# The down projection of a gated MLP written as seven products of halves (Strassen) in place of one direct product

## The chip, the cores and the metric

One core of one Trainium2 chip. The metric is the device time of one execution in microseconds (us). The engines are named as in the profile: PE is the matrix engine (PEld its weight loads), DVE the vector engine, ACT the scalar engine, POOL the GpSimd engine, SP the engine that issues nearly all transfers.

## The reference

One layer of a hybrid token mixer followed by a gated MLP with a depthwise convolution, for 512 tokens of 1024 channels, in fp32. The part that matters here is the second half:

```python
def conv_ffn(h, p):
    u, g = jnp.split(h @ p['ffn_w_up'], 2, axis=-1)
    g = depthwise_conv(g, p['ffn_conv_w'], p['ffn_conv_b'])
    return (jax.nn.silu(g) * u) @ p['ffn_w_down']
...
x = x + gate2 * conv_ffn(ada_norm(x, norm2_g, shift2, scale2), p)
out = rmsnorm(x, final_norm_g)
```

(the last two lines are shortened.) `ffn_w_up` is 1024 x 5632, `ffn_w_down` is 2816 x 1024. So the down projection is a product of 512 x 2816 activations with 2816 x 1024 weights.

## The kernel before, in words

All fp32 products are made of three matmuls of a rounded type: each operand x is split into a high part (a cast on ACT) and a low part (x minus the high part, on DVE), and high-high, high-low and low-high are added in PSUM (`mm3`, L99; `split`, L95). A weight tile is loaded by SP into one of 2 raw buffers and split into one of 3 buffers for each part (`load_split`, L84), so the split of a tile waits until PE has read the tile three places ahead of it.

The MLP starts at L996. The normalised input is kept channel by channel as `hxh` and `hxl` (L179), 8 tiles of 128 channels x 512 tokens each, and the residual stream as 8 tiles `xt` in the same layout. The **up projection** makes 44 tiles of 128 hidden channels (22 of `g`, 22 of `u`), each of 8 x 3 matmuls of 512 columns (`up`, L1015). The first three tiles (L1023) are done by token halves, since the second half of the input is ready later. For each of the 22 hidden tiles (loop at L1032), the convolution reads the `g` tile (one ACT and two DVE instructions), SiLU follows on ACT, the `u` tile is multiplied in on DVE, and the result is split into `act`. Accumulators are in PSUM: 4 banks for large products (tag `big`: `pup`, `pdn` and others) and 4 for all others (tag `ps`) (L74).

The **down projection** (loop at L1045) goes over 8 tiles of 128 output channels. Weights are the stationary operand, the 512 tokens of `act` stream past:

```python
1045        for mt in range(KT):
...
1050            for hs in ((full,) if mt < KT - 1 else halves):
1051                p = ps("pdn")[:, hs]
1052                for k in range(NF):
1053                    wh, wl = ws[k // KT]
1054                    w = slice((k % KT) * P, (k % KT + 1) * P)
1055                    mm3(p, wh[:, w], wl[:, w], act[k][:, 0, hs], act[k][:, 1, hs], k == 0, k == NF - 1)
```

That is 7 tiles of 22 x 3 matmuls of 512 columns and one, the last, of 2 x 22 x 3 of 256 columns. After each tile the residual is added, its squares are summed over the tiles (`ssq`), the final norm's gain is multiplied in (`xg`), and PE transposes the tile to token rows (`pxt`, 4 transposes), which ACT copies into `xo` (4 tiles of 128 tokens x 1024 channels). At the end each token half has its sum of squares formed by PE (`pst`), a chain of small instructions gives the reciprocal root, and the rows are scaled and stored (4 transfers of 512 KB, L1081).

The order of the instructions on each engine is set by a planner when the kernel is built: the program text gives priorities, and an instruction may move ahead of earlier ones that are not ready by the planner's own costs. Stretches marked `pinned` keep the order of the text. Transfers issued by one engine go out in that engine's order, and one that waits holds up those behind it.

Of the kernel before, what the change touches and what calls it, by code (L numbers as in the profile page):

```python
# [14 lines left out]
P = 128  # L15
# [6 lines left out]
EPS = 1e-6  # L22
FH = 2816
NF = FH // P
GW = 64
RW = 63

# [12 lines left out]
INV2PI = 1.0 / (2 * math.pi)  # L40
MAGIC = 1.5 * 2.0 ** 23
PI_LO = 3.1415925
CUT = 576


@with_exitstack
def block_kernel(ctx: ExitStack, tc: tile.TileContext, A):
# [47 lines left out]
    def split(hi, lo, src):  # L95
        S.copy(hi, src)
        V.tensor_sub(lo, src, hi.bitcast(F32))
# [18 lines left out]
    def col(name, i=0, n=1):  # L116
        o = COLS[name][0] + i
        return cols[:, o:o + n]
# [877 lines left out]
    with ExitStack() as ff:  # L996
        fp = ff.enter_context(tc.tile_pool(name="ffn", bufs=1))
        h2h, h2l = hxh, hxl

        def tmp(n):  # L1000
            return yslot("hm", dt=F32)[:, 0, :n]

        for h, hs in enumerate(halves):
            if h:
                norm2_cols(h)
                norm2_rows(h)
            for k in range(KT):
                modulate(tmp, h2h[:, k, hs], h2l[:, k, hs], xt[k][:, hs], rb2[h], a2col[:, k:k + 1], modc[:, 8 + k:9 + k])
        act = []
# [12 lines left out]

        first = {}  # L1023
        for m in (NF, 0, NF + 1):
            first[m] = (load_split(A["wup"][m], name="wup"), ps("pup"))
        for hs in halves:
            for ms in ((NF, 0), (NF + 1,)):
# [4 lines left out]
        for f in range(NF):  # L1032
            pg = first[NF + f][1] if NF + f in first else up(NF + f)
            gt = fp.tile([P, T], F32, name="gt", tag="gt", bufs=2)
# [8 lines left out]
        xo = fp.tile([P, 4, D], F32, name="xo")  # L1043
        tmp = temp(fp)
        for mt in range(KT):  # L1045
            ws = []
            for c in range(0, NF, KT):
                n = min(KT, NF - c)
                ws.append(load_split(A["wdn"][mt, :, c * P:(c + n) * P], n * P, name="wdn"))
            for hs in ((full,) if mt < KT - 1 else halves):  # L1050
                p = ps("pdn")[:, hs]
                for k in range(NF):
                    wh, wl = ws[k // KT]
                    w = slice((k % KT) * P, (k % KT + 1) * P)
                    mm3(p, wh[:, w], wl[:, w], act[k][:, 0, hs], act[k][:, 1, hs], k == 0, k == NF - 1)
                V.scalar_tensor_tensor(xt[mt][:, hs], p, modc[:, 24 + mt:25 + mt], xt[mt][:, hs], ALU.mult, ALU.add)
                n = hs.stop - hs.start
                if mt < KT - 1:
                    sumsq(tmp, ssq[:, hs], xt[mt][:, hs], mt == 0)
                else:  # L1060
                    sq = tmp(n)
                    S.activation(sq, xt[mt][:, hs], AF.Square)
                xg = fp.tile([P, T], F32, name="xg", tag="gt", bufs=2)[:, hs]
                V.tensor_scalar(xg, xt[mt][:, hs], col("final", mt), None, ALU.mult)
                tt = range(4)[hs.start // P:hs.stop // P]
                if mt == KT - 1:
                    r = rms_cols(sum_cols(ssq[:, hs], sq))
                pt = ps("pxt")[:, hs]
                for i in range(len(tt)):
                    PE.transpose(pt[:, i * P:(i + 1) * P], xg[:, i * P:(i + 1) * P], ident)  # L1070
                if mt == 4:
                    preload_sqrt(ssq[:, 0:1])
                if mt < KT - 1:
                    S.copy(xo[:, tt.start:tt.stop, mt * P:(mt + 1) * P], pt.rearrange("p (t c) -> p t c", c=P))
                    continue
                for i, t in enumerate(tt):
                    rt = r[:, i:i + 1]
                    V.tensor_scalar(xo[:, t, :CUT], xo[:, t, :CUT], rt, None, ALU.mult)
                    S.mul(xo[:, t, CUT:mt * P], xo[:, t, CUT:mt * P], rt)
                    V.tensor_scalar(xo[:, t, mt * P:], pt[:, i * P:(i + 1) * P], rt, None, ALU.mult)  # L1080
                    nc.sync.dma_start(A["out"][t * P:(t + 1) * P], xo[:, t])  # L1081

# [52 lines left out]
def _arrays(x, c, ctx, c_ctx, w_mod, b_mod, norm1_g, norm2_g, w_in, pool_w, pool_scale,  # L1135
            hyena_conv_w, hyena_conv_b, hyena_filt_w1, hyena_filt_b1, hyena_filt_w2,
            hyena_filt_b2, hyena_filt_w3, hyena_filt_b3, hyena_freq, hyena_skip, na_rpb,
            w_branch, w_out, ffn_w_up, ffn_conv_w, ffn_conv_b, ffn_w_down, final_norm_g):
    import numpy as np
    a = _constants()  # L1140

    def tcol(v):
        return v.reshape(-1, P).T

    def chan(m):
        return m.T.reshape(KT, P, -1).transpose(1, 0, 2)
# [20 lines left out]
    a["wdn"] = mtiles(ffn_w_down[0])  # L1167
# [46 lines left out]
```

## Time and profile before

| | us |
|---|---|
| median of 3 runs | 855.87 (855.58 to 857.28) |
| the profiled execution | 855.23 |
| its span, first to last instruction | 853.4 |
| mixer and output projection | up to about 475 |
| MLP, up projection | about 475 to 718 |
| MLP, down projection | 718 to 843.5 |
| from there to the end | 9.9 |

PE is busy 832.1 of the 853.4 us, DVE 502.6, ACT 332.1. Matmuls are pipelined: the duration shown for one (376 ns on average) is longer than the step from one to the next, so what PE can do is read from start to start, or from a long unbroken stretch and its count. The same holds in a smaller measure for instructions of DVE.

### The profile page before, as it was taken

The page shows a single profiled execution, that of the slowest core. Times are in us where ns is not written, and L with a number is a line of the kernel's source. Part 1 is how long each engine was busy: PE and PEld are TensorE (multiplying, and loading weights), DVE is VectorE, ACT ScalarE, POOL GpSimd, SP SyncE. Part 2 cuts the span into 40 slices and gives each one's busy share as a digit, 9 for nine tenths or more (in the row PEclk, how much of TensorE's full clock was granted, in tenths as well). Part 3 has the DMA queues.
Part 4 walks back from the last instruction along what each step waited for, and adds up shares of the span by engine and source line. Part 5 has one row for each costly group of instructions (what it writes and reads, how often), then busy time and mean ns, then how long its engine had stood idle before and what let it go on. Part 6 is the DMA issues. An engine that isn't in the chain of part 4 may idle for free.

```text
span 853.4 us, 10736 instructions
## 1 busy us (share of the span) xinstructions
PE 832.1 (97%) x4192; PEld 683.8 (80%) x4192; DVE 502.6 (59%) x874; ACT 332.1 (39%) x519; POOL 5.9 (1%) x16
## 2 busy tenths in 40 slices
PE   6999999989999999999999999999999999999995
PEld 2577888868888888888889988888888888888885
DVE  4879998699797863445444964444444444232333
ACT  6634452625454332323333453333333333222321
POOL 0100000000000000000000000000000000000000
PEclk9999999999999999999999999999999999999998
DMA  8912314645656542223332233222222333332312
GB/s 315 414 60 74 99 44 140 190 144 208 210 166 220 185 158 93 93 93 130 113 122 76 74 124 99 98 97 92 91 96 95 99 99 93 87 107 84 93 57 99
DMA packets 30363, 107.31 MB, mean 126 GB/s; under 512 B 3783, under 2 KB 4935, under 8 KB 29288
## 3 DMA queue, kind: packets, MB, share of 16 engines
q1 hardware_dynamic: 30312, 106.62, 37.6%
q8 instruction: 33, 0.54, 0.3%
q14 instruction: 18, 0.15, 0.0%
HBM read 104.51 MB, written 2.10 MB: 125 GB/s over the span
## 4 chain that ended last, share of the span: by engine, by line
PE 86%; DVE 8%; ACT 2%; DMA 1%; issue 1%; SPq 0%; DVEq 0%; ACTq 0%
PE pup L60 28%; PE pin L60 25%; PE pdn L60 14%; PE pwo L60 5%; PE pbr L60 5%; PE pss L60 1%; DVE za L60 1%; PE pKe L60 1%; PE pav L60 1%; DVE winl L60 1%; DVE zb L60 1%; PE pmod L60 1%; DMA cb<-in_crow_dram 1%; DMA wm<-in_wmB_dram 1%; DVE wgl L60 1%
## 5 line engine op out<-in xcount | busy, mean ns | idle before, releaser
L60 PE MATMUL pup<-hxh,wupl 128*128 128x512 f32 (+1 forms) x376 | 140.8, 376 | 0.0
L60 PE MATMUL pup<-hxl,wuph 128*128 128x512 f32 (+1 forms) x376 | 140.6, 376 | 0.0
L60 PE MATMUL pup<-hxh,wuph 128*128 128x512 f32 (+1 forms) x376 | 139.9, 376 | 0.7 <-ACT wuph L60 0.4
L60 PE MATMUL pdn<-act,wdnh 128*128 128x512 f32 (+1 forms) x396 | 112.7, 368 | 0.0
L60 PE MATMUL pin<-hxh,wgh 128*128 128x512 f32 x256 | 101.2, 395 | 0.6 <-ACT wgh L60 0.6
L60 PE MATMUL pin<-hxh,wgl 128*128 128x512 f32 x256 | 100.3, 392 | 0.0
L60 PE MATMUL pin<-hxl,wgh 128*128 128x512 f32 x256 | 100.2, 391 | 0.0
L60 DVE TENSOR_TENSOR wupl<-wupr,wuph 128x1024 fp32r<-128x1024 f32 x44 | 53.9, 1225 | 71.7 <-ACT wuph L60 69.8
L60 ACT CAST wuph<-wupr 128x1024 fp32r<-128x1024 f32 x44 | 46.3, 1053 | 92.6 <-PE pup L60 90.2
L60 PEld LDWEIGHTS pdn<-act,wdnh 128*128 128x128 f32 x396 | 71.6, 189 | 12.0
L60 PEld LDWEIGHTS pup<-hxh,wupl 128*128 128x128 f32 x376 | 70.7, 188 | 13.1 <-DVE wupl L60 0.2
L60 PEld LDWEIGHTS pup<-hxh,wuph 128*128 128x128 f32 x376 | 70.1, 188 | 13.7 <-ACT wuph L60 0.6
L60 PEld LDWEIGHTS pup<-hxl,wuph 128*128 128x128 f32 x376 | 70.6, 188 | 12.8
L60 PE MATMUL pdn<-act,wdnl 128*128 128x512 f32 (+1 forms) x198 | 72.4, 366 | 0.0
L60 DVE TENSOR_TENSOR wdnl<-wdnr,wdnh 128x1024 fp32r<-128x1024 f32 (+1 forms) x24 | 27.2, 1134 | 63.3 <-ACT wdnh L60 63.2
L60 ACT ACTIVATE sg<-pin 128x512 f32<-128x512 f32 x32 | 19.2, 600 | 113.5 <-PE pin L60 113.4
L60 DVE SCALAR_TENSOR_TENSOR sg<-sg,pbr 128x512 f32<-128x512 f32 x24 | 16.5, 689 | 75.8 <-PE pbr L60 75.8
L60 PEld LDWEIGHTS pin<-hxh,wgh 128*128 128x128 f32 x256 | 48.1, 188 | 10.5 <-ACT wgh L60 1.0
L60 PEld LDWEIGHTS pin<-hxh,wgl 128*128 128x128 f32 x256 | 48.1, 188 | 10.3 <-issue 0.5
L60 PEld LDWEIGHTS pin<-hxl,wgh 128*128 128x128 f32 x256 | 48.1, 188 | 9.8 <-issue 0.5
L60 ACT CAST wdnh<-wdnr 128x1024 fp32r<-128x1024 f32 (+1 forms) x24 | 23.6, 983 | 72.5 <-PE pdn L60 66.7
L60 PE MATMUL pin<-hxh,winh 128*128 128x512 f32 x128 | 51.7, 404 | 0.0
(265 smaller groups left out, 1427.5 us busy)
## 6 DMA issues: line engine op xcount, KB each, us to landing
wupr<-in_wup_dram SPq DMA_DIRECT2D x44, 512.0 KB, 3.4
wgr<-in_wg_dram SPq DMA_DIRECT2D x32, 640.0 KB, 3.9
wm<-in_wmB_dram SPq DMA_DIRECT2D x32, 512.0 KB, 4.6
wm<-in_wmA_dram SPq DMA_DIRECT2D x8, 1024.0 KB, 9.9
winr<-in_win_dram SPq DMA_DIRECT2D x16, 512.0 KB, 3.5
wdnr<-in_wdn_dram SPq DMA_DIRECT2D x16, 512.0 KB, 3.5
wor<-in_wout_dram SPq DMA_DIRECT2D x8, 512.0 KB, 3.5
wdnr<-in_wdn_dram SPq DMA_DIRECT2D x8, 384.0 KB, 3.1
```

The lines of the kernel that those rows point to most:

```text
L60: ins = f(*a, **k)
```

## The change

The hidden channels are halved (11 tiles each), the tokens are halved (2 x 256) and the output channels are halved (2 x 512). Seven products of 256 x 1408 by 1408 x 512 take the place of the eight of the direct form. In each, 128 x 128 blocks of the activations are the stationary operand, and 512 columns of the weights stream past; a product fills two PSUM banks (two blocks of 128 tokens). Write A for the first hidden half and B for the second, 1 and 2 for the token halves, W11 to W22 for the quarters of the weights (hidden half, output half).

- p7: (A1 - A2) with W12 + W22. p6: (A2 - B2 - A1) with W12 + W22 + W11. p4: B2 with the sum of all four. These three run hidden tile by hidden tile beside the up projection (`part`, taken by `run_part` from a queue `todo` between the up tiles: three per pair of hidden tiles, from the second pair on). The summed weights of a hidden tile lie in one buffer (`chain`): one transfer on SP loads W12, three transfers issued by POOL each add a quarter to it in memory; two of the three are issued after the sum so far has been split.
- p1: A1 with W11. p5: (A2 - B2) with W11 + W12. p2: B1 with W21. p3: (A2 - B2 - A1 + B1) with W22. These follow the up projection, in chunks of two hidden tiles (`product`). W12 is added onto W11 in place by POOL's transfers after W11 has been split.
- The residual is transposed to token rows early (after the first up tiles) instead of the result at the end; the output halves are formed from the products' PSUM banks on DVE (`usum`, `y21`, `y22`, `y11`, `y12`), the gate's row is spread over the partitions by 8 small matmuls (`g2_row`), and the squares are summed along rows on ACT.
- The up projection's accumulators share their 4 banks with p4 (2 banks) from the second pair on.

The diff, cut to its core:

```diff
-    hxh = hp.tile([P, KT, T], F32R, name="hxh")
-    hxl = hp.tile([P, KT, T], F32R, name="hxl")
...
+            self.t = [hp.tile([P, KT // 2, T], F32R, name=f"hx{2 * i + j}") for j in range(2)]
...
-        for m in (NF, 0, NF + 1):
+        for m in (NF, 0, NF + NH):
...
+        for mt in range(KT):
+            pt = ps("pxt")
+            for i in range(4):
+                PE.transpose(pt[:, i * P:(i + 1) * P], xt[mt][:, i * P:(i + 1) * P], ident)
+            S.copy(xo[:, :, mt * P:(mt + 1) * P], pt.rearrange("p (t c) -> p t c", c=P))
...
+        def prod(b, ah, al, w, k, tts=(0, 1)):
+            for t in tts:
+                c = slice(t * P, (t + 1) * P)
+                PE.matmul(b[t], ah[:, c], w[0], start=k == 0, stop=False)
+                PE.matmul(b[t], ah[:, c], w[1], start=False, stop=False)
+                PE.matmul(b[t], al[:, c], w[0], start=False, stop=k == NH - 1)
...
+        def chain_load(k):
+            chain[k] = fp.tile([P, T], F32, name="ch", tag="ch", bufs=2)
+            nc.sync.dma_start(chain[k], A["wdq"][0, 1, :, k])
+            nc.gpsimd.dma_start(chain[k], A["wdq"][1, 1, :, k], accum_op=ALU.add)
...
+        def part(j, k):
+            r, b = chain[k], (p7, p6, p4)[j]
+            w = wsplit(r)
+            if j < 2:
+                nc.gpsimd.dma_start(r, A["wdq"][j, 0, :, k], accum_op=ALU.add)
+            if k == 0:
+                b.extend(ps("pdn" if j == 2 else "pda") for _ in range(2))
+            prod(b, tps[k][:, j, 0], tps[k][:, j, 1], w, k)
+        def run_part(keep=2):
+            if len(todo) > keep:
+                part(*todo.pop(0))
...
             S.activation(gt, gt, AF.Silu)
+            run_part()
             pu = first[f][1] if f in first else up(f)
             V.tensor_mul(gt, gt, pu)
-            act.append(yslot("act") if f < 8 else fp.tile([P, 2, T], F32R, name="act", tag=f"act{f}"))
-            split(act[f][:, 0], act[f][:, 1], gt)
...
+        def half_pair(k):
...
+            V.tensor_sub(s1[:, 0], g1[:, :TC], g1[:, TC:])
+            split(tps[k][:, 0, 0], tps[k][:, 0, 1], s1[:, 0])
...
+            split(pers[k][:, 0, :TC], pers[k][:, 1, :TC], g1[:, :TC])
+            todo.append((0, k))
+        def pair(k):
...
+            V.tensor_sub(s1[:, 0], g1[:, TC:], g2[:, TC:])
+            V.tensor_sub(s1[:, 1], s1[:, 0], g1[:, :TC])
+            split(tp[:, 1, 0], tp[:, 1, 1], s1[:, 1])
+            split(tp[:, 2, 0], tp[:, 2, 1], g2[:, TC:])
+            split(sg[0][:, :TC], sg[1][:, :TC], s1[:, 0])
+            V.tensor_add(s1[:, 1], s1[:, 1], g2[:, :TC])
+            split(sg[0][:, TC:], sg[1][:, TC:], s1[:, 1])
+            split(pers[k][:, 0, TC:], pers[k][:, 1, TC:], g2[:, :TC])
+            todo.extend(((1, k), (2, k)))
+        chain_load(0)
+        for k in range(NH):
+            if k < NH - 1:
+                chain_load(k + 1)
+            hidden(k)
+            half_pair(k)
+            run_part()
+            hidden(NH + k)
+            pair(k)
+            if k < NH - 1:
+                run_part()
+        while len(todo) > 1:
+            run_part(0)
...
+        def y21(t):
+            V.tensor_add(vv[t], u[:, t], p7[t])
+            V.tensor_add(m, vv[t], p4[t])
+            resid(2 + t, lo_, m)
+            sumsq2(2 + t, 0)
+        def y11(t):
+            V.tensor_add(e1[:, t], e1[:, t], p2[t])
+            resid(t, lo_, e1[:, t])
+            sumsq2(t, 0)
+            V.tensor_mul(xo[:, t, lo_], xo[:, t, lo_], gfb[:, lo_])
...
+        then = {c: [call(add_w12, ks)] for c, ks in enumerate(chunks)}
+        then[3].append(call(run_part, 0))
+        p1 = product("pdn", ..., w11, then=then)
+        p5 = product("pda", ..., lambda ks: t1s[ks[0] // 2],
+                     then={1: [call(usum, 0)], 2: [call(usum, 1)], 3: [call(y21, 0)], 4: [call(y21, 1)]})
+        p2 = product("pdn", ..., w21,
+                     then={1: [call(y22, 0)], 2: [call(y22, 1)], 3: [call(preload_sqrt, sqs[:, 2, 0:1])]})
+        p3 = product("pda", ..., w22, 3,
+                     then={0: [call(y11, 0)], 1: [call(y11, 1)], 2: [call(y12, 0)], 3: [call(y12, 1)]})
...
+        V.tensor_mul(ms[1], p3[1], g2b[:, hi_])
+        V.tensor_add(xo[:, 1, hi_], xo[:, 1, hi_], ms[1])
+        rstd_b(0)
+        sumsq2(1, 1)
+        last_scale(0)
+        rstd_a(1, 1)
+        rstd_b(1)
+        last_scale(1)
```

`resid` multiplies by the gate's row and adds to `xo` (two DVE instructions); `sumsq2` is one ACT instruction; `last_scale` scales one half of a row block on ACT and the other on DVE and stores it. `product(..., 3, ...)` runs the last three chunks of p3 for the first 128 tokens, then for the second.

## Rows read from the trace of the kernel before

**Rows 1.** The page, its first part: busy time of PE.
```profile
PE 832.1 (97%) x4192; PEld 683.8 (80%) x4192; DVE 502.6 (59%) x874; ACT 332.1 (39%) x519; POOL 5.9 (1%) x16
```

**Rows 2.** Windows: length, PE, PEld, DVE, ACT, POOL busy (x), PEclk, DMA share, GB/s.
```profile
484.84:718.22 233.38, 233.38 (x1071) 195.00 (x1071) 116.95 (x145) 90.96 (x118) 0.00 (x0) 1.00 0.30 97
718.22:843.52 125.30, 125.30 (x635) 106.08 (x633) 40.34 (x56) 33.59 (x43) 0.00 (x0) 1.00 0.29 85
843.52:853.40 9.88, 1.12 (x9) 0.87 (x8) 3.28 (x12) 1.64 (x4) 0.00 (x0) 0.73 0.27 107
```

**Rows 3.** The chain of waits, in order of time: start, length, what.
```profile
484.24 0.60 PE pb L60 x4
484.84 233.38 PE pup L60 x1070
...
767.08 0.44 PE pxt L60 x4
767.52 14.98 PE pdn L60 x66
...
835.76 0.62 PE pst L60 x6
```

**Rows 4.** Timeline of PE in the last down tile: start, length, instruction.
```profile
842.60 0.40 PE L60 MATMUL pdn<-act,wdnh 128*128 128x256 f32 x2
...
842.96 0.40 PE L60 MATMUL pdn<-act,wdnh 128*128 128x256 f32 x2
```

**Rows 5.** Groups of PE by shape, down projection: count, busy and mean, idle before.
```profile
L60 PE MATMUL pdn<-act,wdnh 128*128 128x512 f32 x308 | 96.5, 391 | 0.0
L60 PE MATMUL pdn<-act,wdnl 128*128 128x512 f32 x154 | 59.9, 389 | 0.0
L60 PE MATMUL pdn<-act,wdnh 128*128 128x256 f32 x88 | 16.2, 286 | 0.0
L60 PE MATMUL pdn<-act,wdnl 128*128 128x256 f32 x44 | 12.4, 283 | 0.0
```

**Rows 6.** Groups of DVE and ACT by shape: up projection, the last one earlier.
```profile
L60 DVE TENSOR_TENSOR wupl<-wupr,wuph 128x1024 fp32r<-128x1024 f32 x38 | 46.5, 1225 | 65.6 <-ACT wuph L60 63.7
L60 ACT CAST wuph<-wupr 128x1024 fp32r<-128x1024 f32 x38 | 40.1, 1054 | 85.0 <-PE pup L60 85.0
L60 DVE SCALAR_TENSOR_TENSOR gt<-pup,cols,gt 128x511 f32<-128x511 f32 x36 | 26.9, 747 | 0.6
L60 DVE TENSOR_TENSOR act<-gt,act 128x512 fp32r<-128x512 f32 x20 | 13.6, 685 | 0.0
L60 DVE TENSOR_TENSOR za<-zb 128x256 f32<-128x256 f32 x16 | 5.9, 421 | 0.0
```

**Rows 7.** Timeline of DVE: two independent instructions, one behind the other.
```profile
708.24 1.22 DVE L60 TENSOR_TENSOR wdnl<-wdnr,wdnh 128x1024 fp32r<-128x1024 f32 x1
...
709.38 0.69 DVE L60 TENSOR_TENSOR act<-gt,act 128x512 fp32r<-128x512 f32 x1
```

**Rows 8.** DVE after the last matmul, and the stores.
```profile
843.52 0.48 DVE L60 SCALAR_TENSOR_TENSOR x<-pdn,modc,x 128x256 f32<-128x256 f32 x1 [4.21 <-PE pdn L60]
...
846.08 0.16 DVE L60 TENSOR_TENSOR rt<-rr 128x2 f32<-128x2 f32 x1
...
847.99 0.35 DVE L60 TENSOR_SCALAR xo<-pxt,rr 128x128 f32<-128x128 f32 x1
...
DMA to landing us min/median/max: 2.7/3.0/4.2
```

**Rows 9.** Transfers: count, KB each, median us from issue to landing.
```profile
x<-in_xT_dram SPq DMA_DIRECT2D x8, 256.0 KB, 3.7
...
tabI<-in_tabI_dram SPq DMA_DIRECT2D x1, 512.0 KB, 11.0
rc<-in_rcnt_dram SPq DMA_DIRECT2D x2, 256.0 KB, 2.8
```

More of the change, by code (lines that the diff above doesn't have):

```diff
@@ new lines, in wsplit @@
+        def wsplit(raw):
+            n = raw.shape[-1]
+            hi = wp.tile([P, WCH], F32R, name="wdnh", tag="wh")[:, :n]
+            lo = wp.tile([P, WCH], F32R, name="wdnl", tag="wl")[:, :n]
+            split(hi, lo, raw)
+            return hi, lo
+        def chain_load(k):
+            chain[k] = fp.tile([P, T], F32, name="ch", tag="ch", bufs=2)
+            nc.sync.dma_start(chain[k], A["wdq"][0, 1, :, k])
+            nc.gpsimd.dma_start(chain[k], A["wdq"][1, 1, :, k], accum_op=ALU.add)
@@ new lines, in part, with hidden @@
+        def part(j, k):
[9 more added lines that the diff above has]
+                part(*todo.pop(0))
+        gts = {}
+        def hidden(f):
@@ L1040, in block_kernel @@
-            split(act[f][:, 0], act[f][:, 1], gt)
[L1043 to L1081, printed above, removed]
@@ new lines, in pair @@
+        def pair(k):
+            g1, g2 = gts.pop(k), gts.pop(NH + k)
+            tp = tps[k]
+            sg = [xtile("sg", T, F32R) if k < 4 else fp.tile([P, T], F32R, name="sg", tag=f"sg{k}{i}") for i in range(2)]
+            s1 = fp.tile([P, 2, TC], F32, name="s1", tag="s1", bufs=1)
+            V.tensor_sub(s1[:, 0], g1[:, TC:], g2[:, TC:])
[6 more added lines that the diff above has]
+            split(pers[k][:, 0, TC:], pers[k][:, 1, TC:], g2[:, :TC])
+            sgs.append(sg)
+            todo.extend(((1, k), (2, k)))
@@ new lines, in block_kernel @@
+        chain_load(0)
[11 more added lines that the diff above has]
+            run_part(0)
+        g2f = hp.tile([P, 2, D], F32, name="g2f", tag="hx0")
+        g2b, gfb = g2f[:, 0], g2f[:, 1]
+        nc.sync.dma_start(gfb, A["finrow"].broadcast_to([P, D]))
@@ new lines, in block_kernel, with wload, place @@
+        chunks = [list(range(c, min(c + 2, NH))) for c in range(0, NH, 2)]
+        e1 = fp.tile([P, 2, T], F32, name="e1", tag="tp", bufs=2)
+        u = fp.tile([P, 2, T], F32, name="u", tag="tp", bufs=2)
+        vv = [fp.tile([P, T], F32, name="vv", tag="ch", bufs=2) for _ in range(2)]
+        def wload(raw, i, j, ks):
+            nc.sync.dma_start(raw, A["wdq"][i, j, :, ks[0]:ks[-1] + 1])
+            return raw
+        pairs = {}
+        def place(q, ks, *tags):
+            c, n = ks[0] // 2, len(ks) * T
+            if c < 2:
+                return wp.tile([P, WCH], F32, name="wdnr", tag="wr", bufs=2)[:, :n]
+            if c % 2 == 0:
+                pairs[q] = hp.tile([P, 2, 2 * T], F32, name="wdnp", tag=tags[c // 2 - 1])
+            return pairs[q][:, c % 2, :n]
@@ new lines, in block_kernel, with w11, w21, w22 @@
+        t1s = []
+        def w11(ks):
+            t1s.append(wload(place(1, ks, "hx1", "hx2"), 0, 0, ks))
+            return t1s[-1]
+        def w21(ks):
+            return wload(place(2, ks, "hx3", "hx1"), 1, 0, ks)
+        def w22(ks):
+            return wload(place(3, ks, "hx2", "hx3"), 1, 1, ks)
+        def add_w12(ks):
+            nc.gpsimd.dma_start(t1s[ks[0] // 2], A["wdq"][0, 1, :, ks[0]:ks[-1] + 1], accum_op=ALU.add)
+        def product(name, x, raws, tail=0, then={}):
+            b = [ps(name) for _ in range(2)]
+            late = []
+            for c, ks in enumerate(chunks):
+                hi, lo = wsplit(raws(ks))
+                for f in then.get(c, ()):
+                    f()
+                for i, k in enumerate(ks):
+                    w = hi[:, i * T:(i + 1) * T], lo[:, i * T:(i + 1) * T]
+                    if c < len(chunks) - tail:
+                        prod(b, *x(k), w, k)
+                    else:
+                        late.append((w, k))
+            for t in range(2):
+                for w, k in late:
+                    prod(b, *x(k), w, k, (t,))
+            return b
@@ new lines, in block_kernel, with resid, sumsq2, g2_row @@
+        lo_, hi_ = slice(0, T), slice(T, D)
+        def resid(t, cs, y):
+            m = fp.tile([P, T], F32, name="m", tag="gt", bufs=3)
+            V.tensor_mul(m, y, g2b[:, cs])
+            V.tensor_add(xo[:, t, cs], xo[:, t, cs], m)
+        sqs = cp.tile([P, 4, 2], F32, name="sqs")
+        def sumsq2(t, j):
+            m = fp.tile([P, T], F32, name="m", tag="gt", bufs=3)
+            S.activation(m, xo[:, t, (lo_, hi_)[j]], AF.Square, accum_out=sqs[:, t, j:j + 1])
+        def g2_row(h):
+            pb = ps("pb")
+            for i in range(4):
+                mt = 4 * h + i
+                dg = cp.tile([P, P], F32, name="dg", tag="dg", bufs=2)
+                V.tensor_scalar(dg, ident, modc[:, 24 + mt:25 + mt], None, ALU.mult)
+                PE.matmul(pb[:, i * P:(i + 1) * P], ones, dg, start=True, stop=True)
+            S.copy(g2b[:, h * T:(h + 1) * T], pb)
@@ new lines, in y12, with call @@
+        def y12(t):
+            resid(t, hi_, u[:, t])
+        def y11(t):
[3 more added lines that the diff above has]
+            V.tensor_mul(xo[:, t, lo_], xo[:, t, lo_], gfb[:, lo_])
+        def call(f, *a):
+            return lambda: f(*a)
+        then = {c: [call(add_w12, ks)] for c, ks in enumerate(chunks)}
+        then[3].append(call(run_part, 0))
+        for t in range(2):
+            then[t].append(call(take6, t))
+            then[2 + t].append(call(g2_row, t))
@@ new lines, in block_kernel @@
+        p1 = product("pdn", lambda k: (pers[k][:, 0, :TC], pers[k][:, 1, :TC]), w11, then=then)
+        p5 = product("pda", lambda k: (sgs[k][0][:, :TC], sgs[k][1][:, :TC]), lambda ks: t1s[ks[0] // 2],
+                     then={1: [call(usum, 0)], 2: [call(usum, 1)], 3: [call(y21, 0)], 4: [call(y21, 1)]})
+        p2 = product("pdn", lambda k: (pers[k][:, 0, TC:], pers[k][:, 1, TC:]), w21,
+                     then={1: [call(y22, 0)], 2: [call(y22, 1)], 3: [call(preload_sqrt, sqs[:, 2, 0:1])]})
@@ new lines, in block_kernel, with rstd_a @@
+        p3 = product("pda", lambda k: (sgs[k][0][:, TC:], sgs[k][1][:, TC:]), w22, 3,
+                     then={0: [call(y11, 0)], 1: [call(y11, 1)], 2: [call(y12, 0)], 3: [call(y12, 1)]})
+        rt = {}
+        def rstd_a(t, j):
+            pre, v, r = (cp.tile([P, 1], F32, name=n, tag=n, bufs=2) for n in ("tp", "tv", "tr"))
+            V.tensor_scalar(pre, sqs[:, t, 1 - j:2 - j], D * EPS, None, ALU.add)
+            V.tensor_scalar(v, sqs[:, t, j:j + 1], pre, 1.0 / D, ALU.add, ALU.mult)
+            S.activation(r, v, AF.Sqrt)
+            rt[t] = v, r
@@ new lines, in rstd_b, with out @@
+        def rstd_b(t):
+            v, r = rt[t]
+            q = cp.tile([P, 1], F32, name="tq", tag="tq", bufs=2)
+            V.reciprocal(r, r)
+            V.scalar_tensor_tensor(q, r, r, v, ALU.mult, ALU.mult)
+            V.tensor_scalar(q, q, -0.5, 1.5, ALU.mult, ALU.add)
+            V.tensor_mul(r, r, q)
+            rt[t] = r
+        def out(t):
+            nc.sync.dma_start(A["out"][t * P:(t + 1) * P], xo[:, t])
+        for t in (2, 3):
+            rstd_a(t, 0)
+            V.tensor_mul(xo[:, t], xo[:, t], gfb)
+            rstd_b(t)
+            S.mul(xo[:, t], xo[:, t], rt[t])
+            out(t)
@@ new lines, in last_scale @@
+        def last_scale(t):
+            S.mul(xo[:, t, lo_], xo[:, t, lo_], rt[t])
+            V.scalar_tensor_tensor(xo[:, t, hi_], xo[:, t, hi_], rt[t], gfb[:, hi_], ALU.mult, ALU.mult)
+            out(t)
+        pinned[0] = True
+        ms = []
+        for t in range(2):
+            ms.append(fp.tile([P, T], F32, name="ml", tag="ch", bufs=2))
+        V.tensor_mul(ms[0], p3[0], g2b[:, hi_])
+        V.tensor_add(xo[:, 0, hi_], xo[:, 0, hi_], ms[0])
+        sumsq2(0, 1)
+        rstd_a(0, 1)
```

36 lines of the change are left out of this document (30 added, 6 removed).

## The prediction

> **What bounds the kernel now.** I read the busy times first: PE is busy 832.1 of 853.4 us [rows 1]. That alone says little, since a matmul's shown duration is longer than its step. So I went on to the windows of the MLP [rows 2]: from 484.84 to 843.52 PE is busy for the whole of both stretches (233.38 of 233.38, 125.30 of 125.30), at granted clock 1.00, while DVE works 116.95 and 40.34 us and the transfers take 0.3 of their engines. The chain of waits agrees: it stays on PE through both, and never leaves it for a split or a load [rows 3]. Third, the step: 66 matmuls of 512 columns take 14.98 us [rows 3], so one costs 0.227 us, not the 0.39 us that the groups show [rows 5]. The up stretch gives nearly the same, 233.38 us for 1070 matmuls of which few are half width. In the last tile three matmuls of 256 columns start 0.36 us apart (842.60 to 842.96 [rows 4]): 0.120 each, more than half of 0.227. PE has no gap to be closed, so only fewer or cheaper matmuls shorten this part, and whatever makes PE wait lengthens it.
>
> **The change, part by part.**
>
> *Matmuls.* Before: 308 + 154 = 462 of 512 columns and 88 + 44 = 132 of 256 [rows 5]: 462 x 0.227 + 132 x 0.120 = 104.9 + 15.8 = 120.7 us. After: seven products x 11 hidden tiles x 2 token blocks x 3 = 462 of 512 columns, 104.9 us. So the seven full tiles cost what the seven products cost, and the eighth tile goes: **-15.8**. I assume the step stays 0.227 when weights stream and activations are stationary; shapes and types are the same.
>
> *Small PE work.* The transposes, 8 sets of 4 at 0.44 us or a little more [rows 3], stay, but the last set leaves the end for the start of the MLP. The column sums go (0.62 for one half within the down stretch [rows 3], the other half is in the tail), 8 small matmuls for the gate's row come, two sets like the 0.60 of the set of four [rows 3]. Against the down stretch's 125.30 [rows 2], the new work is 104.9 + 8 x 0.46 + 1.2 = 109.8. **Together -15.5 on PE**, all of it on the path.
>
> *DVE and ACT beside the up projection.* Per pair of hidden tiles DVE has 4 weight splits of 1.225, 4 convolution steps of 0.747, 2 products of 0.685, 3 splits of summed weights of 0.685 and 11 half-width sums and splits of 0.421 [rows 6]: 4.9 + 3.0 + 1.4 + 2.1 + 4.6 = 16.0 us. PE needs (96 + 18) x 0.227 = 25.9. ACT worked 90.96 of 233.38 [rows 2], about 8.2 us a pair; even at 1.054 [rows 6] for each of its 8 added casts it stays below 17. Both are covered by the matmuls. If one stalled, PE would come to wait at the next weight split, which is made at most two tiles ahead.
>
> *PSUM.* The up projection has 2 of its 4 banks left from the second pair on. A `g` bank is read by one ACT and two DVE instructions (about 0.8 + 2 x 0.747), while PE fills the other bank for 24 x 0.227 = 5.4 us and runs a part of 1.4. Covered: 0, with the upper bound 2.5 us in the one iteration where the banks change owner. I put 0.3 for this and for the early transposes' 8 copies on ACT.
>
> *Transfers.* The weights of the down projection are read twice (23 MB for 11.5), on transfer engines used to 0.3 [rows 2]. SP's queue gets 11 loads of summed weights in front of up-weight loads; a buffer is asked for a pair early, so SP must wait for a part's split, but a raw up buffer is likewise refilled some two tiles (12 us) before use. New to this kernel are transfers that add in memory, issued by POOL: 33 of 256 KB and 6 of up to 512 KB. No row has one. The nearest are plain 256 KB loads of 2.8 and 3.7 us; the farthest is 11.0, a load in a crowded stretch [rows 9]. I take 3.7 as the nearest in size, with the ends 2.8 and 11.0. Cover: between parts 0 and 1 of a tile PE runs one up tile and one part, 6.8 us; the split before it is normally ready as much earlier, so some 11 us when splits run ahead, 5.5 when they don't. Cost at 3.7: 0.
>
> No transfer of this kernel is issued by POOL, so no run so far shows what the Trainium skill says here (SBUF - State Buffer, Who interferes with whom): a DVE instruction in a mode that uses both of its port pairs keeps GpSimd from writing descriptors until it ends. By that rule an add could be held for one DVE instruction at a time, and on a DVE that is 60% busy it would cost the chain extra; it speaks against the change. The Trainium skill also gives (DMA: Bandwidth & Descriptors, Anatomy of one DMA) 2.0 us + bytes / 436 GB/s, an estimate of 2.6 us for 256 KB, and the sum by it would be the same.
>
> *Where the up projection ends.* After the last up matmul DVE must do a product, 8 half-width sums and splits, a part's split and the first chunk's split of p1: 0.685 + 3.4 + 0.685 + 1.225 = 6.0 us, or 5.2 by the steps between independent instructions (1.14 from 708.24 to 709.38 for one shown at 1.22 [rows 7]). PE has three parts in hand, 18 x 0.227 = 4.1. **+1.2** (0 to 2).
>
> *The last three products.* PE: 3 x 66 x 0.227 = 45.0 us. DVE: 16 chunk splits not made ahead, 18.0; 32 full-width sums at 0.685, 21.9; the norms of two row blocks, 4.4. That is 44.3 us at shown durations, about 39 by steps. DVE goes from a third of the stretch (40.34 of 125.30) to nearly all of it. The worst place is the start of p3: the third chunk's split stands behind both `y11` (8 x 0.685 = 5.5), ready at 6.7 us where PE has 24 matmuls, 5.4, in hand. **+1.5** (0, to 4.0 if only one chunk was ready ahead).
>
> *The tail.* Before: 843.52 to 848.34, 4.8 us of short steps, then two stores close together, landing in up to 4.2 [rows 8]; 9.88 in all [rows 2]. After: two full-width steps (1.4), four small ones of the other row block (0.16 each [rows 8], 0.2 with what lies between), its scaling 0.7, two small, the root 0.25, four small, scaling 0.7: 5.0. The last store then runs alone, nearer the 2.7 to 3.0. **-0.9** (-1.5 to +1).
>
> *Sum.* 855.23 - 15.5 + 0.3 + 1.2 + 1.5 - 0.9 = 841.8 against the profiled execution, which lies 0.64 below the median of 855.87; so **842.5** as a median.
>
> **The rivals.**
>
> *All of it arrives.* DVE's order hides both stalls: 842.5 - 2.7, about 840. For it: DVE's sum by steps is 39 of 45.
>
> *DVE becomes the bound of the last products*, or the up stretch loses some tenths per pair: 4 us at p3, 2 at the end of the up projection, 0.3 for each of 11 pairs: some 846 to 849. For it: 44.3 of 45.0 at shown durations, instructions that depend on each other gain nothing from overlap, and an in-order queue has no reserve at that load. Against it: up to p1, DVE is at 16 of 25.9.
>
> *The adding transfers decide, and it is slower.* Place: part 1 of each hidden tile waits for an add that was issued only after part 0's split, and since ACT and DVE take splits in order, the up splits behind it wait too. Nothing is lost below the cover of 5.5 to 11 us. Above it each of 11 tiles loses the excess; 13.4 us are gone at 1.2 each, so at landings of 6.7 to 12.2 us the gain is used up, and at 11.0 with the short cover it is 842.5 + 11 x 5.5 = 903. For it: no row shows such a transfer, DVE is busy, and the planner places parts by its own costs. Against it: 256 KB land in 2.8 and 3.7, the stretch has only 97 GB/s [rows 2]. By the Trainium skill's rule above the holds come on top.
>
> *It does not do what it says*: the step is longer with streaming weights. At 0.262 in place of 0.227 in 462 matmuls all is eaten and the time is the same. Rows of both stretches show one step for two kinds of streamed operand, so this is unlikely.
>
> **How the numbers follow.** A measurement of this kernel can tell a difference of about 0.2%, 1.7 us. Chances: forecast 0.60 (841 to 845), all of it arrives 0.13, DVE bound 0.14, adding transfers 0.11 (a small part of it still faster or the same), step 0.02. Faster 0.87, same 0.03, slower 0.10. The range takes in the full gain at 839.5 and most of the DVE case, to 849; left out is what is slower or the same, some 0.15 with the far end of the DVE case.
>
> **What would show it.** In the changed profile: 462 matmuls into `pdn` and `pda` and none of 256 columns into them; a step of 0.227; the up stretch longer by the parts in it, 30 x 1.36 = 41 us; PE without waits until the last up tile; a wait of 1 to 2 us there on a split and one at p3's third chunk; DVE near full from p5 on; the adds landing in under 5 us; a tail of 9. I am wrong if PE waits for `chain` splits during the up projection, if those transfers take over 7 us, if the step changes, or if PE waits more than 5 us in the four last products.

## The result, and the profile after

The changed kernel takes **842.6 us** as the median of 4 runs (842.25 to 843.87), against 856.13 (855.58 to 857.28) for the kernel before on the same chip: a ratio of **0.9843 (0.9826 to 0.986)**. Its profiled execution took 842.34, with a span of 840.6. The forecast was 842.5, from a profiled 841.8. Run again later in five rounds, the same kernel gave 841.3, ratio 0.9831 (0.9818 to 0.9845), so one median of it is good to about 1 us and no better.

The busy times of the page, to be laid beside [rows 1]:

```profile
PE 816.9 (97%) x4060; PEld 667.7 (79%) x4060; DVE 561.5 (67%) x1032; ACT 369.8 (44%) x623; POOL 39.8 (5%) x55
```

PE has 15.2 us less, DVE 58.9 more. The seven products are 462 matmuls, all of 512 columns, as forecast. Next the windows of the MLP in the changed kernel, to be laid beside [rows 2]. The columns are window, length, then busy time and count of PE, PEld, DVE, ACT and POOL, the granted clock of PE, the share of the transfer engines and GB/s. The cuts are: the up projection with the parts of p7, p6 and p4 in it, its end, p5, p2, p3, and the tail.

```profile
486.31:764.44 278.13, 278.13 (x1283) 232.17 (x1283) 160.74 (x270) 124.98 (x208) 25.91 (x30) 1.00 0.49 121
764.44:786.30 21.86, 21.83 (x101) 17.23 (x101) 12.77 (x24) 11.92 (x18) 6.05 (x7) 1.00 1.03 258
786.30:801.37 15.07, 15.07 (x68) 12.39 (x67) 13.17 (x18) 9.18 (x14) 0.00 (x0) 1.00 0.71 214
801.37:816.33 14.96, 14.96 (x67) 12.39 (x67) 14.71 (x29) 7.75 (x13) 0.00 (x0) 1.00 0.36 117
816.33:831.50 15.17, 15.17 (x66) 11.96 (x65) 13.37 (x20) 7.51 (x12) 0.00 (x0) 1.00 0.18 70
831.50:840.60 9.10, 0.00 (x0) 0.00 (x0) 4.58 (x15) 2.56 (x6) 0.00 (x0) 0.76 0.28 115
```

PE is busy for the whole of every stretch but the tail, at granted clock 1.00, as before. So the gain is fewer matmuls and not fewer gaps; there were none to close. DVE, a third of the down stretch before [rows 2], now has 13.17 of 15.07, 14.71 of 14.96 and 13.37 of 15.17 us in the three last products. Where the up projection ends, the transfers fill their engines (1.03).

The chain of waits of the changed kernel from the MLP's start, in order of time (start, us, what), answers to [rows 3]:

```profile
478.00 1.57 PE pup L60 x11
...
496.61 3.62 PE pxt L60 x32
...
505.71 1.65 PE pda L60 x6
...
545.48 10.88 PE pup L60 x48
556.36 1.36 PE pdn L60 x6
...
563.16 1.36 PE pda L60 x6
...
773.09 0.44 PE pb L60 x4
...
773.79 0.71 PE pb L60 x4
...
778.40 0.45 PE pb L60 x4
...
779.78 0.58 PE pb L60 x4
...
786.30 15.07 PE pda L60 x66
801.37 14.96 PE pdn L60 x66
816.33 12.91 PE pda L60 x56
```

The chain does not leave PE between the first up tile and the last product (it shows no wait for another engine or a transfer there, and one gap of 0.03). From the second part on, six matmuls cost 1.36 wherever they stand among the up tiles, and p2's 66 cost 14.96: 0.227 each, the step of [rows 3]. The 32 transposes take 3.62, the gate's row four sets of 0.44 to 0.71.

The adding transfers and the loads beside them, from the list of transfer issues of the changed kernel (count, size, median us to landing):

```profile
wupr<-in_wup_dram SPq DMA_DIRECT2D x44, 512.0 KB, 4.1
...
ch<-in_wdq_dram POOLq DMA_DIRECT2D x33, 256.0 KB, 4.2
...
ch<-in_wdq_dram SPq DMA_DIRECT2D x11, 256.0 KB, 3.4
...
wdnp<-in_wdq_dram POOLq DMA_DIRECT2D x3, 512.0 KB, 10.4
...
wdnr<-in_wdq_dram POOLq DMA_DIRECT2D x2, 512.0 KB, 9.7
```

An add of 256 KB lands in 4.2 us, 0.8 later than the plain load of the same size into the same buffer. The five of 512 KB have medians of 9.7 and 10.4; all are issued in the stretch with the share of 1.03.

**Where the time went.** From the chain's first up matmul to the end of the last matmul the MLP took 367.0 us before (476.52 to 843.52) and takes 353.5 now (478.00 to 831.50): -13.5. The tail went from 9.88 [rows 2] to 9.10: -0.8. Together -14.3. But the MLP began 1.48 later in this execution, and that lies far ahead of the changed part: near the program's start two loads stand on its chain that are not on the chain of the kernel before, the second being

```profile
15.51 11.66 DMA winr<-in_win_dram
```

Over the other executions of the changed kernel and its variants profiled in this study, the MLP's start lay between 476.66 and 478.70. The four that began after 478 have the same load on their chain, and no other has. So the span fell by 12.8 and not by 14.3.

### The profile page after: what moved, and what is told of

The parts are those of the page before. It is cut to its first block, busy times and chain, and to the rows that moved or that the text cites. A ratio compares the mean times of both kernels' runs of the same rounds, so it can differ in the third digit from the quotient of the medians.

```text
span 840.6 us, 10896 instructions
## 1 busy us (share of the span) xinstructions
PE 816.9 (97%) x4060; PEld 667.7 (79%) x4060; DVE 561.5 (67%) x1032; ACT 369.8 (44%) x623; POOL 39.8 (5%) x55
## 4 chain that ended last, share of the span: by engine, by line
PE 85%; DVE 8%; DMA 3%; ACT 2%; issue 1%; SPq 1%; DVEq 0%; ACTq 0%
PE pup L60 29%; PE pin L60 26%; PE pda L60 7%; PE pdn L60 5%; PE pwo L60 5%; PE pbr L60 5%; DMA winr<-in_win_dram 1%; DVE za L60 1%; PE pav L60 1%; PE pKe L60 1%; DMA fw<-in_fw_dram 1%; DVE winl L60 1%; DVE zb L60 1%; SPq L60 1%; DMA cb<-in_crow_dram 1%
## 5 line engine op out<-in xcount | busy, mean ns | idle before, releaser
L60 PE MATMUL pup<-hx,wuph 128*128 128x512 f32 (+1 forms) x752 | 220.0, 376 | 0.7 <-ACT wuph L60 0.4
L60 PE MATMUL pin<-hx,wgh 128*128 128x512 f32 x512 | 160.7, 393 | 0.6 <-ACT wgh L60 0.6
L60 PEld LDWEIGHTS pup<-hx,wuph 128*128 128x128 f32 x752 | 138.1, 188 | 26.7 <-ACT wuph L60 0.6
L60 PE MATMUL pup<-hx,wupl 128*128 128x512 f32 (+1 forms) x376 | 140.8, 376 | 0.0
L60 PEld LDWEIGHTS pin<-hx,wgh 128*128 128x128 f32 x512 | 95.0, 188 | 20.3 <-ACT wgh L60 1.0
L60 PE MATMUL pin<-hx,wgl 128*128 128x512 f32 x256 | 100.3, 392 | 0.0
L60 PE MATMUL pin<-hx,winh 128*128 128x512 f32 x256 | 81.4, 398 | 0.0
L60 PEld LDWEIGHTS pup<-hx,wupl 128*128 128x128 f32 x376 | 70.7, 188 | 12.9 <-DVE wupl L60 0.2
L60 PEld LDWEIGHTS pin<-hx,wgl 128*128 128x128 f32 x256 | 48.1, 188 | 10.3 <-issue 0.5
L60 DVE TENSOR_TENSOR gt<-gt,pup 128x512 f32<-128x512 f32 x22 | 15.1, 687 | 54.4 <-PE pup L60 50.2
L60 PE MATMUL pin<-hx,winl 128*128 128x512 f32 x128 | 50.5, 395 | 0.2 <-DVE winl L60 0.2
## 6 DMA issues: line engine op xcount, KB each, us to landing
wm<-in_wmA_dram SPq DMA_DIRECT2D x8, 1024.0 KB, 11.1
```

The lines of the kernel that those rows point to most:

```text
L60: ins = f(*a, **k)
```

## The experiments

All medians are beside 856.1 to 856.7 for the kernel before on the same chip. A change is taken against 842.6 and against 841.3, the two medians of the changed kernel, where the difference matters. "The MLP" is the time from the chain's first up matmul to the end of the span: 362.6 in the changed kernel's first profile, 362.3 when it ran again.

### Matmuls taken away beside the up projection, and put back behind it

**p4 without its middle parts** (54 matmuls fewer, all among the up tiles):

```diff
-            prod(b, tps[k][:, j, 0], tps[k][:, j, 1], w, k)
+            if j < 2 or k in (0, NH - 1):
+                prod(b, tps[k][:, j, 0], tps[k][:, j, 1], w, k)
```

> Edit: the third part (p4) keeps its weight splits and its sums, but 9 of its 11 hidden tiles issue no matmuls: 54 matmuls of 512 columns fewer beside the up projection; that part of the computation is left out. If PE sets the pace there (my theory), the time falls by 54 x 0.227 = 12.2 us, to about 830.4. If the splits on ACT and DVE or the adding transfers set the pace of that stretch (rival), it falls by less than 4, to 839 or more.

Measured: 829.74, ratio 0.9689 (0.9673 to 0.9705), 12.9 below 842.6 and 11.6 below 841.3; 54 x 0.2267 is 12.2. The matmuls beside the up projection are on the path at very nearly full price, so neither DVE, the transfers nor PSUM set the pace there. (The MLP is 350.8 long, 11.5 to 11.8 less; the chain now leaves PE once, for 2.4 us that are mostly DVE's work, at the end of the up projection.)

**The eighth product put back** (the nine middle hidden tiles of p2 are multiplied in twice):

```diff
                         prod(b, *x(k), w, k)
+                        if raws is w21 and 0 < k < NH - 1:
+                            prod(b, *x(k), w, k)
```

> Edit: 9 of p2's 11 hidden tiles issue their matmuls twice, so 54 of the 66 matmuls of an eighth product are there again, with no further splits, loads or sums (those tiles count twice). If the whole gain is the eighth product's matmuls and the new order is neutral in itself (my theory): + 54 x 0.227 = 12.3, 854.9. If part of the gain comes from the new order, or the added matmuls run beside DVE's work at no cost (rival), it stays below 850.

Measured: 854.41, ratio 0.9982 (0.9969 to 0.9994), 13.1 above the 841.3 of the unchanged kernel on the same chip. One line of this kernel's chain says it:

```profile
802.85 27.20 PE pdn L60 x120
```

120 matmuls in 27.20 are again 0.2267 each; 54 of them are 12.2. The rest of the 13.1 is not theirs: 0.9 more went by ahead of p5, where this execution's chain waits for a load of W11,

```profile
764.21 8.43 DMA wdnp<-in_wdq_dram
```

which the unchanged kernel's does not. All else of the change stands (the sums, the adds, the streamed weights), and 12.2 of the 14.8 us of gain (856.15 to 841.3) are gone with the 54 matmuls; the other 12 of an eighth product would be 2.7 more, an estimate by the same step. So the missing product's matmuls are the gain, within the 1 us that a median is good for.

### What is next behind PE in the last products

**p2 without its middle hidden tiles** (the same 54 matmuls fewer, behind the up projection):

```diff
+                    if raws is w21 and k not in (0, NH - 1):
+                        continue
                     if c < len(chunks) - tail:
                         prod(b, *x(k), w, k)
```

> Edit: the product p2 keeps all its splits and sums, but 9 of its 11 hidden tiles issue no matmuls: 54 matmuls of 512 columns fewer in the last products, as many as in the run beside it; that part of the computation is left out. If PE alone sets the pace there with DVE just below it (my theory: DVE 41.3 of 45.2 us busy in p5, p2 and p3), DVE takes over after some 4 us and the time falls by 3 to 6, to about 838. If DVE has room to spare it falls by 12.2, to 830.4; if DVE sets the pace already (rival), by less than 1.5.

Measured: 841.79, ratio 0.9833 (0.9816 to 0.985). That lies between the two medians of the changed kernel: nothing gained, where 3 to 6 us were expected. From p5's start to the end this kernel takes 54.8 us and the changed one 54.3. Two of its windows, columns as above:

```profile
801.40:810.00 8.60, 3.00 (x8) 1.36 (x6) 8.60 (x12) 5.87 (x10) 0.00 (x0) 0.70 0.40 113
809.04:812.38 3.34, 3.29 (x7) 2.21 (x8) 3.16 (x5) 1.62 (x3) 0.00 (x0) 0.50 0.64 227
```

and one line of its chain:

```profile
812.38 5.20 PE pda L60 x17
```

Where p2's matmuls are missing, DVE is busy for the whole of the 8.60 us and PE for 3.00. The granted clock is 0.70 in this window and 0.50 in the next, the lower of PE's two levels (1.2 and 2.4 GHz), and when PE is full again, 17 matmuls take 5.20, 0.306 each. So DVE takes over, and the lower clock makes the matmuls behind it dearer. How much of the 12.2 us each of the two took is not shown by this run: from 817.7 to 828.7 the chain runs over DVE's instructions again.

**Less work on DVE** (the gate's row is not multiplied in ahead of the tail, and the final norm's gain only on the second output half of the first two row blocks; all matmuls stay):

```diff
-            m = fp.tile([P, T], F32, name="m", tag="gt", bufs=3)
-            V.tensor_mul(m, y, g2b[:, cs])
-            V.tensor_add(xo[:, t, cs], xo[:, t, cs], m)
+            V.tensor_add(xo[:, t, cs], xo[:, t, cs], y)
...
-            V.tensor_mul(xo[:, t, lo_], xo[:, t, lo_], gfb[:, lo_])
...
-            V.tensor_mul(xo[:, t], xo[:, t], gfb)
```

> Edit: in the output sums the multiplications by the gate's row and by the final norm's gain are left out (except in the tail of the last half): 8 + 2 DVE instructions of 512 columns and 2 of 1024, some 9 us of DVE work, gone from p5, p2 and p3; that part of the computation is left out. If PE sets the pace and DVE just fits beside it (my theory), the time stays within 1 us of 842.6. If DVE sets the pace of these products (rival), it falls by 2 to 9 us.

Measured: 842.15, ratio 0.9842 (0.9813 to 0.987): no change. The windows of p5, p2 and p3 in it:

```profile
786.82:801.89 15.07, 15.07 (x67) 12.40 (x67) 11.88 (x16) 9.21 (x14) 0.00 (x0) 1.00 0.69 214
801.89:816.85 14.96, 14.96 (x67) 12.39 (x67) 12.56 (x27) 9.19 (x14) 0.00 (x0) 1.00 0.44 152
816.85:831.93 15.08, 15.06 (x66) 12.04 (x65) 8.98 (x13) 6.26 (x12) 0.00 (x0) 1.00 0.09 36
```

DVE falls from 41.25 to 33.42 us in the three, and they take the same time. In the changed kernel DVE costs nothing there, although it is 98% busy in p2.

**Both edits together:**

> Edit: the run without p2's 54 matmuls and the run without the multiplications, together; both parts of the computation are left out. Without the matmuls alone the time was 841.8. If DVE's in-order work was what took over there (my theory), it now falls by 5 to 9 us, to 833 to 837. If PE's lower granted clock or something else holds it (rival), it stays above 840.

Measured: 837.06, ratio 0.9775 (0.9757 to 0.9793): 4.7 below p2's cut alone. So DVE was what had taken over in that run. From p5's start to the end it is 50.2 us for 54.3, 4.1 of the 12.2. Where the rest went, a window and one line of the chain show:

```profile
800.00:808.95 8.95, 3.46 (x12) 2.21 (x11) 8.95 (x12) 7.00 (x10) 0.00 (x0) 0.84 0.48 150
```

```profile
810.66 15.70 PE pda L60 x64
```

DVE, with its work cut, is still busy for the whole of 8.95 us while PE has 3.46, and then 64 matmuls take 15.70 in place of 14.5, the first of them at the lower clock again (granted clock 0.50 from 808.95 to 810.66). The chain puts 3.40 us down to a load of W22, but DVE has no idle time in that window, and no instruction from 796 to 826 waited for a transfer; so the load held nothing up. Behind PE it is DVE in this stretch. What would come after DVE isn't shown.

### The adding transfers

**No adds** (the weights are then single quarters and not sums; the loads on SP stay):

```diff
-            nc.gpsimd.dma_start(chain[k], A["wdq"][1, 1, :, k], accum_op=ALU.add)
...
-            if j < 2:
-                nc.gpsimd.dma_start(r, A["wdq"][j, 0, :, k], accum_op=ALU.add)
...
-            nc.gpsimd.dma_start(t1s[ks[0] // 2], A["wdq"][0, 1, :, ks[0]:ks[-1] + 1], accum_op=ALU.add)
```

> Edit: all 39 adding transfers are left out, so the summed weights are single quarters; the sums of the weights are left out of the computation. If the adds are covered (my theory) the time stays within 1 us of 842.6. If they hold up splits or the queue somewhere (rival), it falls by 2 us or more.

Measured: 841.3, ratio 0.9827 (0.9812 to 0.9841), the very median of the changed kernel run again, and its MLP is 362.3 too. The adds cost nothing, all 39 of them.

**Each of the 22 later adds three times, and two times:**

```diff
-            if j < 2:
+            for _ in range(3 if j < 2 else 0):
```

(with 2 in place of 3 in the second kernel)

> Edit: each adding transfer that follows a part's split is made three times, one behind the other, so the next part's weights come some 8.4 us later (each lands in 4.2 us median); the quarters added count three times. With the long cover of about 11 us between one part and the next (my theory), 12.6 us is too late by some 1 to 3 us for each of 10 hidden tiles: +5 to +30 us, 848 to 873. With the short cover of 5.5 us it is 10 x 7, +70 us. If the adds never matter, 0.

> Edit: each adding transfer that follows a part's split is made twice, one behind the other; the quarters added count twice. From the run with three: a hidden tile took 35.1 us there with six adds of about 4.5, so 8 us of other steps in the loop; the loop closes within the 25.8 us that PE needs if an add takes less than about 9. Two adds in a row are 9.0: 842.6 to 850 (theory of the closed loop). With the short cover of 5.5 us for each add it would be 22 x 3.5, some 920.

Measured: three times 955.81, ratio 1.1164 (1.1147 to 1.118), 113 us more, beyond both expectations; two times 880.93, ratio 1.0287 (1.0268 to 1.0307), 38 us more, between them. Both expectations of each run missed, so the cover was sized wrongly. What the loop is can be read in the chain of the kernel with two adds, which no longer runs over PE:

```profile
561.44 4.50 DMA ch<-in_wdq_dram
...
566.22 4.13 DMA ch<-in_wdq_dram
570.43 0.63 ACT wdnh L60
571.09 0.70 DVE wdnl L60
...
572.08 4.01 DMA ch<-in_wdq_dram
...
576.38 7.66 DMA ch<-in_wdq_dram
...
584.63 1.05 ACT wuph L60
585.71 1.23 DVE wupl L60
586.93 0.67 DVE gt L60
...
588.47 0.64 ACT gt L60
...
589.74 0.70 DVE wdnl L60
```

From one split of part 0 (its end at 561.15) to the next (590.44) a tile takes 29.29 us, where the changed kernel needs 25.84. Its four adds are 20.30 of that. The other 9.0 are splits and, in ACT's and DVE's order, what stands behind the last of them: the cast of an up weight, its low part, the convolution, SiLU, and only then the split of the next tile's part 0, which releases the next add. So the adds behind part 0 and those behind part 1 lie in **one** loop, although the program text chains only the adds of one tile. Nothing is lost while the loop is shorter than PE's 25.84 per tile; above, every tile loses the whole excess. ACT's waits on these transfers show the same: 132.2 us in 20 waits with two adds, 2.3 us in one in the changed kernel.

The sum comes in two parts. The split of part 0 starts on ACT in the second and in the tenth of the 11 tiles at these times, first in the changed kernel, then with two adds:

```profile
530.33 0.62 ACT L60 CAST wdnh<-ch 128x512 fp32r<-128x512 f32 x1 [0.96 <-PE pup L60]
...
737.05 0.62 ACT L60 CAST wdnh<-ch 128x512 fp32r<-128x512 f32 x1 [0.92 <-PE pup L60]
```

```profile
530.95 0.62 ACT L60 CAST wdnh<-ch 128x512 fp32r<-128x512 f32 x1 [0.96 <-PE pup L60]
...
763.84 0.61 ACT L60 CAST wdnh<-ch 128x512 fp32r<-128x512 f32 x1
```

That is 25.84 and 29.11 a tile, so eight tiles lose 26.2. From the first up matmul to p5's start the kernel with two adds took 39.1 us more than the changed one (347.4 for 308.3). The other 13.0 are lost behind the tenth tile, where the up projection runs out: PE has no matmul left and stands idle for 11.14 us while two adds in a row of the last tile land (791.0 to 803.0).

```profile
804.09 1.22 PE L60 MATMUL pda<-wdnh,tp 128*128 128x512 f32 x2 [11.14 <-ACT tp L60]
```

With three adds a tile took 35.75 (531.85 to 817.84); of the 113.6 us to p5's start, 79.3 were lost in these eight tiles, 2.1 ahead of them and 32.2 behind them.

### The tail and the gate's row

**p3 without its reordered end** (the last three chunks no longer finish the first token block ahead of the second):

```diff
-        p3 = product("pda", lambda k: (sgs[k][0][:, TC:], sgs[k][1][:, TC:]), w22, 3,
+        p3 = product("pda", lambda k: (sgs[k][0][:, TC:], sgs[k][1][:, TC:]), w22, 0,
```

> Edit: p3 runs both token blocks hidden tile by hidden tile to its end, in place of one block after the other in its last three chunks. Same matmuls. The chain of the first block is then no longer beside PE's last 3.4 us: two more full-width DVE steps, an ACT step and two small ones on the end path, 1.5 to 3 us: 844 to 845.6. If the end path is not what follows the last matmul, no change.

Measured: 844.18, ratio 0.9863 (0.9845 to 0.9881), 1.6 above 842.6 and 2.9 above 841.3. Its MLP is 2.4 longer, and 1.6 of that is the end: from the start of the last matmul it takes 11.1 us in place of 9.5. The order of the last product keeps that off the tail. The other 0.9 lies ahead of p5, outside the edit, where this execution's chain waits for a load of W11 (8.60) as in the kernel with the eighth product.

**An attempt at a better version** (a third buffer for the diagonal blocks of the gate's row, and the last row block's root ahead of the other's scaling):

```diff
-                dg = cp.tile([P, P], F32, name="dg", tag="dg", bufs=2)
+                dg = fp.tile([P, P], F32, name="dgr", tag="dgr", bufs=3)
...
-        last_scale(0)
         rstd_a(1, 1)
+        last_scale(0)
         rstd_b(1)
```

> Edit: the gate row's diagonal blocks get three buffers of their own in place of two shared ones, and in the tail the last block's variance steps stand ahead of the scaling of the block before it. Same computation. If the end path is the chain seen in the trace, the second edit takes 0.4 to 0.7 us off it and the first 0.3 to 0.6 us of PE's interruptions: 841.3 to 842. If the diagonal blocks made early hold up the norm on DVE at the start of the MLP instead, no gain or a small loss.

Measured: 841.55, ratio 0.9835 (0.9821 to 0.9849), against 841.3 for the changed kernel on the same chip: no gain. The last matmul's start to the end fell by about 0.4 as hoped (9.0 from 9.4 to 9.5), but 1.2 us more went by between the first up matmul and the last, 0.2 of it at the MLP's start, where the planner now put the diagonal blocks on DVE ahead of the norm. The other 1.0 lies at the end of the up projection, where a load of W11 (8.93) is waited for as in the two executions above whose edits lie elsewhere; so whether this edit costs or gains some tenths of a us isn't shown.

**The changed kernel again**, as the measure for the small differences:

> The changed kernel itself, unchanged, beside the two that follow on one chip: 842.6 again within 1.5 us by either theory.

Measured: 841.3, as above; its MLP began at 476.69 and took 362.3.

## Why the prediction was right, and by how much of it luck

*The bound and the price per matmul* held. PE has no gap before or after, and 54 matmuls are worth 11.6 to 13.1 us in either direction for 12.2 by the step of [rows 3]. The step with streaming weights is 0.227 to the third digit, so the rival of a longer step is out. (Its price was a little off: in 462 matmuls the 13.4 us of the sum are gone at a step of 0.256; 0.262 would cost 16.2.)

*Small PE work:* the transposes came as put (3.62 for 8 sets, 0.45 each for 0.46). The gate's row was mis-sized: 0.44 + 0.71 + 0.45 + 0.58 = 2.2 where I put 1.2. The four sets come apart, since the diagonal blocks have two buffers; I had counted matmuls where the length came from the step between DVE and PE. **+1.0** that I did not have.

*The 0.3 for the start:* the first part takes 1.65 where later ones take 1.36. Right.

*The end of the up projection:* 84 matmuls (19.0) and the gate's row (2.2) fill 21.2 of 21.86. So 0.6 was lost where I put 1.2.

*The last three products:* DVE is as full as I summed it, 41.25 of 45.2 where I had 39 by steps and 44.3 at shown durations. But the stall at p3 that I put at 1.5 did not come. The DVE timeline of the changed kernel at that place (start, duration, engine, line, operation):

```profile
815.82 0.68 DVE L60 TENSOR_TENSOR e<-e,pdn 128x512 f32<-128x512 f32 x1
816.41 1.22 DVE L60 TENSOR_TENSOR wdnl<-wdnr,wdnh 128x1024 fp32r<-128x1024 f32 x1
817.55 0.68 DVE L60 TENSOR_TENSOR m<-e,g2f 128x512 f32<-128x512 f32 x1
...
819.35 1.22 DVE L60 TENSOR_TENSOR wdnl<-wdnp,wdnh 128x1024 fp32r<-128x1024 f32 x1
```

I had let the third chunk's split stand behind all eight instructions of `y11`. Only one chunk was split ahead of p3's start at 816.33, the case that I priced at 4.0. But `y11` began before p2 had ended, and the planner put a split after the first of the eight instructions and the next after three more: the second chunk's at 816.41, the third chunk's at 819.35. That one is done at 820.6, where PE asks for it at 816.33 + 24 x 0.227 = 821.8. PE never waited. The failure is one of reading: the text's order of work is not DVE's order in a kernel where a planner may move a ready instruction ahead. So two rivals share the truth: PE stays the bound as forecast, and at p3 "all of it arrives". That DVE is right behind PE, the core of the third case, is shown by the cut of p2, which gained nothing.

*The adding transfers:* cost 0 as put; the landing is 4.2 for the 3.7 I took. The rival that carried most of the risk was priced wrongly, though. I counted one add per tile against a cover of 5.5 or 11 us; the runs show two adds per tile in one loop, and a cover of (25.84 - 9.0) / 2 = 8.4 us for each. By that loop the gain of 14.8 us would be used up when 11 x (2 x landing + 9.0 - 25.84) reaches it, at landings of about 9.1 us, an estimate from these rows; with what the kernel with two adds lost behind its tenth tile it would be somewhat earlier. That lies inside the 6.7 to 12.2 that I gave, but by a different sum. The longest landing of 256 KB into that buffer was 7.8 in the changed kernel, and the 512 KB adds of the crowded stretch have medians of 9.7 and 10.4, so I don't call the chance of 0.11 too high.

Whether DVE's work delays an add, which I had feared, the kernel with two adds shows. Its windows over the four adds of one tile, each from issue to landing (the second ends at the next split, 0.1 later):

```profile
561.44:565.94 4.50, 4.50 (x22) 3.72 (x21) 3.61 (x9) 1.82 (x4) 0.86 (x1) 1.00 0.94 149
566.22:570.43 4.21, 4.21 (x20) 3.51 (x19) 0.00 (x0) 0.00 (x0) 0.86 (x1) 1.00 0.59 125
572.08:576.09 4.01, 3.49 (x14) 2.25 (x14) 3.94 (x6) 2.85 (x5) 0.86 (x1) 1.00 0.59 83
576.38:584.03 7.65, 7.65 (x35) 6.31 (x35) 0.92 (x3) 0.00 (x0) 0.86 (x1) 1.00 0.59 157
```

With DVE idle (0.00) an add lands in about 4.1, with DVE busy for 3.94 of 4.01 us in 4.01, and the slowest one, 7.65, has DVE nearly idle (0.92). POOL's issue takes 0.86 in all four, beside TENSOR_TENSOR instructions in the first and beside two SCALAR_TENSOR_TENSOR in the third. So DVE's work delays none of them; why the fourth is slow isn't shown. The Trainium skill (SBUF - State Buffer, Who interferes with whom) says that TENSOR_TENSOR has no mode that takes both port pairs; the first of the four windows agrees, and no run here shows the hold that I had taken from that page. For 256 KB the fit in the Trainium skill (DMA: Bandwidth & Descriptors, Anatomy of one DMA) gives an estimate of 2.6 us, short of the 4.2 measured; the measurement decides.

*The tail:* 9.10 for 9.0. The stores of the last two row blocks left 2.2 us apart and landed in 2.6 and 2.7, at the bottom of [rows 8], as put.

*The sum:* the MLP became 14.3 us shorter where I had 13.4. The stalls were 2.1 too large and the gate's row 1.0 too small; the tail and roundings make up the rest. That the profiled execution still came out at 842.34 is owed to the MLP's start, 1.48 us later in that execution: luck. The median's agreement within 0.1 is luck in part as well, since the same kernel gave 841.3 later, 1.2 below the forecast. Both lie inside the likeliest case; the shorter MLP (855.23 - 14.3 = 840.9) points towards "all of it arrives".

## What to carry to other kernels

Where PE has no gap, count matmuls and multiply by the step from a long unbroken stretch: here that alone gave the gain to 1.5 us (15.8 for 14.3), and added work on DVE, ACT and the transfers cost under 1 us as long as it fitted. Before going on from such a gain, take matmuls away as a test: it shows which engine is next (here DVE, at 98% in p2) and that the same cut can be worth 12 us at one place and nothing at another. For a chain of dependent transfers look at the orders of all engines that its consumers run on, since an in-order queue can close two short chains into one loop, which is free up to PE's time per round and costs all of the excess after it, and more where PE's cover ends.

## What the runs showed of the hardware

A transfer that adds 256 KB onto a buffer in on-chip memory lands in 4.2 us beside a plain load's 3.4 (medians), and in the tile shown of the kernel with two adds the second was issued 4.3 and 4.8 us behind the first. In a stretch with the transfer engines full, adds of 512 KB have medians of 9.7 and 10.4, where up-weight loads of that size have 4.1 over the kernel; plain loads of that size took 8.4 to 8.9 in the same stretch of four executions, so the crowd explains most of it and not the adding. When PE ran out of matmuls for 5.6 us in the last products (3.00 busy of 8.60), the granted clock fell to 0.50 in the stretch behind it, and the next 17 matmuls cost 0.306 each in place of 0.227.
